# A hybrid decoder layer on one core: three sets of small transposes move from TensorE to VectorE and DRAM

## The chip, the core and the metric

The kernel runs on one core of one Trainium2 chip. The metric is the device time of one execution in microseconds (us), taken as the median of several runs. The profile comes from one execution that was recorded by the hardware profiler. Engines are called as the profile calls them: PE is TensorE (matmuls and transposes; PEld is the weight load that overlaps them), DVE is VectorE, ACT is ScalarE, POOL is GpSimd, SP is SyncE, which issues nearly all DMAs.

## What is computed

One decoder layer on a 1024 x 1024 activation in float32. Cut to what matters here:

```python
h = rmsnorm(x, norm1_w);  proj = h @ w_in
# mixer A: gated DeltaNet, 4 heads of 128
o_a = gated_delta_rule(qa, ka, va, g, beta)                # chunked, a state is carried on
o_a = rmsnorm(o_a, gdn_norm_w) * silu(z)                   # per head; z is a slice of proj
# mixer B: 8 heads of 64, (window, dilation) in (128,1),(512,4),(2048,16)
out = (num_0*w_0 + num_1*w_1 + num_2*w_2) / den_tot        # softmax merged over three branches
x = x + concat(o_a, o_b) @ w_out
h = rmsnorm(x, norm2_w);  u = causal_dwconv(h @ w_up);  gate, up = split(u)
x = x + (silu(gate) * up) @ w_down;  return rmsnorm(x, final_norm_w)
```

## The kernel before

**Products.** Matrix products are made of float32 factors split into a rounded high and a low part, so that one product is three matmuls of 128x128 by 128x512 (`xhi,whi`, `xlo,whi`, `xhi,wlo`). The input projection has 24 column blocks of 48 such matmuls: k, V, q, v for the two mixers, eight blocks a (queries and keys of attention), and last four blocks z (the gates of mixer A, one for each head). They are called projection matmuls below. The output projection (`ohi`, `olo`) follows, then an up-projection of 22 rounds (products P1 to P7 of each round, names T, B, A, S, pair) and a down-projection.

**What sets the order.** The program is written as generators that a planner (class `Weave`, L49) interleaves. It keeps a planned TensorE clock, and for every other engine and for the DMA queue a planned time at which it is free (`account`, L81): each operation is charged a fixed time plus a time for each element of a partition. For the DMA queue of SyncE the charge is 0.05 us + 0.00142 us for each element of a partition (L157), and what it writes is ready 2.2 us later. A generator of high priority says how long it would have to wait (`need`, L98; `until` L101 waits for a named event); until then generators of lower priority run, and the lowest are the projection's matmuls. They are what fills TensorE while softmax or a recurrence is under way on the other engines. The order on each engine is fixed when the program is built.

**Mixer A.** Chains of the gated delta rule (L844) run for four heads. A chain ends with `vtok`, tokens on partitions, scaled on GpSimd. `finish` (L913) turns it: per head eight PE transposes into two PSUM banks, two ACT copies `ot` (128x512) that multiply by the norm's weight `gw2`, and a DMA each to `mixer[h]` in DRAM. When a head's z block is done (L585 waits for the event ("o", h)), `og` is loaded from `mixer[h]` (L610) and multiplied by silu(z) (`zz`, L611). `mixer_splits` (L1119) then splits each of the eight mixer outputs into `ohi` (ACT) and `olo` (DVE). These go into the sixteen slots that the projection's `xhi`, `xlo` have held, so they can only be made when the last projection block has used a slot.

**Attention** (L946). Four pairs of heads (pi), two groups each, so eight groups n = 0 to 7, and two steps of two query blocks in a group. `advance` (L1071) is a pipeline of three stages. For a pair of blocks it issues `scores` (L958: products kT,qT, then on DVE two masked reduces per block into `sm` and its maximum, on ACT two exponentials that also sum the denominators `den`, L984); one step later `turn` (L1000: transposes `ident,sm` on PE, copies `pt`, `pb` to SBUF by DVE and ACT in halves, reciprocal of `den`, and a GpSimd copy `rd` that broadcasts the reciprocals to 128x128); one more step later `spread` (L1023: one transpose `ident,rd` for each block into bank `rb`, and after the fourth an ACT copy `rT`), `values` (L1032), `merge_classes` (L1042) and `give` (L1056: `oT` = result times `rT` on DVE, and a DMA to `mixer[4+pi]`). Scores and turned blocks share PSUM banks, so the next scores need the copies `pt`, `pb` of the blocks before.

**Second norm.** In the first round of `up` (L1316) `rms2_power` (L1236) sums squares by sixteen small products and makes 1/rms on DVE and GpSimd (`rs`, tokens on partitions); after P7 `rms2_spread` (L1245) turns it by eight PE transposes, and two DVE copies make `rstdB` (128x1024). After P7 an ACT copy (`u3`) reads the bank `pa` in which P4 goes on adding.

Of the kernel before, what the change touches and what calls it, by code (L numbers as in the profile page):

```python
# [15 lines left out]
P = 128  # L16
# [131 lines left out]
def hybrid_layer(tc, I, out):  # L148
# [110 lines left out]
    vpark = dp.tile([S, 512], F32, name="vpark")  # L259
    qpark = dp.tile([H, P, S], F32, name="qpark")  # L260
    atpark = dp.tile([H, P, S], F32, name="atpark")
    xpark = dp.tile([KT, P, S], F32, name="xpark")
    upark = dp.tile([FT, P, S], F32, name="upark")

# [267 lines left out]
    def dense():  # L532

        yield from wv.until("first")
        yield from wv.until("norms")
        wv.add(2, first_keys())

        srcs, tiles = [], 0
        for col in DENSE:
            if col[0] == "V":  # L540
                srcs += [I["wv"][j] for j in range(4)]
            else:
                srcs.append(I["wi"][tiles])
                tiles += 1
        place = [0]
        raw = [raw_weight(srcs[0])]
        nxt = [weight(None, st=raw.pop())]
        raw.append(raw_weight(srcs[1]))

        def take():  # L550
            w = nxt.pop()
            i = place[0] = place[0] + 1
            if i < len(srcs):
                nxt.append(weight(None, st=raw.pop(), spare=i >= 17))
            if i + 1 < len(srcs):
                raw.append(raw_weight(srcs[i + 1]))
            return w

        def values_by_token(g):

            banks = [bank(t) for t in ("asc", "asc", "ch", "ch")]
            for j in range(4):
                w = [t.rearrange("p (k m) -> p k m", k=2) for t in take()]
                for kk in range(2):
                    k = 2 * j + kk
                    for i, pt in enumerate(banks):
                        c = 4 * g + i
                        yield wv.need(pt, *w)
                        mm3(pt, [t[:, c * P:(c + 1) * P] for t in xs[k]], [t[:, kk, :] for t in w], k == 0, k == KT - 1)
            for i in range(0, 4, 2):  # L570
                vx = A("vx", "ev", shape=(P, 2, 512))
                for e in range(2):
                    c = 4 * g + i + e
                    ac.activation(vx[:, e, :], banks[i + e], AF.Copy, scale=rst[:, c:c + 1])
                c = 4 * g + i
                sy.dma_start(vpark[c * P:(c + 2) * P].rearrange("(e p) d -> p e d", e=2), vx)
            wv.done.add(("V", g))

        for i, col in enumerate(DENSE):
            kind, h = col[:2]  # L580
            if kind == "V":
                yield from values_by_token(h)
                continue
            if kind == "z":
                yield from wv.until(("o", h))  # L585
            w = [t.rearrange("p (k m) -> p k m", k=KT) for t in take()]
            pair = []
            for hh in range(2):
                pt = bank("hf")
                yield wv.need(pt, *w)  # L590
                for k in range(KT):
                    mm3(pt, [t[:, k, :] for t in w], [t[:, half(hh)] for t in xs[k]], k == 0, k == KT - 1)
                    yield 0.0

                pair.append(pt)
                if hh == 0:
                    xr = A("aqkv" if kind == "a" else "xr", "go" if kind == "k" else "ev")
                scaled(pair, "xr", kind == "a", t=xr, hs=(hh,))
            if kind == "k":
                T["k", h] = conv_silu(xr, 4 + h, "kT", "kT*")  # L600
                wv.add(3, kprep(h))
            elif kind == "q":
                q = conv_silu(xr, h, "qT", "qa")
                wv.add(4, qprep(h, q))
            elif kind == "v":
                v = conv_silu(xr, 8 + h, "vT", "qa")
                wv.add(4, vprep(h, v))
            elif kind == "z":
                og = gated[h] = A("og", "kT*")
                sy.dma_start(og, mixer[h])  # L610
                ve.tensor_tensor(og, og, silu2(xr, "zz"), op=OP.mult)  # L611
            else:
                sy.dma_start(apark[h, col[2]], xr)
                wv.done.add(col)
        wv.done.add("dense")
# [295 lines left out]
        wv.add(1, finish(h, vtok))  # L911

    def finish(h, osb):  # L913
        for hh in range(2):
            pt = yield from next_bank("atr", osb)
            for c in range(4):
                i = 4 * hh + c
                tp(pt[:, c * P:(c + 1) * P], osb[:, i * P:(i + 1) * P])
            ot = tile_(sp, [P, 512], F32, "ot", "t2", 2)
            ac.activation(ot, pt, AF.Copy, scale=gw2)  # L920
            sy.dma_start(mixer[h][:, half(hh)], ot)
        wv.done.add(("o", h))


# [21 lines left out]
    def attention():  # L946
        for h in range(2):
            yield from wv.until(("c", h, NCH - 1))
        mk = A("mk", "go", shape=(P, 448))
        sy.dma_start(mk, I["mk"])  # L950
        for h in range(H):
            yield from wv.until(("o", h))
        for g in range(2):
# [46 lines left out]
        def turn(pair):  # L1000
            pts = A("pt", "dv*", shape=(P, 2, 2, 256))
            for b, (it, tag) in enumerate(zip(pair, ("asc", "atr"))):
                sm, near, far, u, den = it["sm"], it["near"], it["far"], it["u"], it["den"]
                nn, nf = near // P, -(-far // P)
                pt = it["pt"] = pts[:, b]
                pps = [bank(tag) for _ in range(2)]
                pvs = [pp.rearrange("p (e i t) -> p e i t", e=2, t=64) for pp in pps]
                for e in range(2):
                    for i in range(nn + nf):
                        o = far + i * P if i < nn else (i - nn) * P  # L1010
                        for pv, rr in zip(pvs, HALVES):
                            tp(pv[:, e, i, :], sm[rr, e, o:o + P], ident[rr, rr], 0.055)
                copies = uv.tensor_copy, lambda dst, src: ua.activation(dst, src, AF.Copy)
                for pv, rr, copy in zip(pvs, HALVES, copies):
                    copy(pt.rearrange("p e (i t) -> p e i t", t=P)[:, :, :nn, rr], pv[:, :, :nn, :])
                    for i in range(nf):
                        rows = min(it["far"] - i * P, P)
                        copy(it["pb"][i][:rows, :, u, rr], pv[:rows, :, nn + i, :])
                rd = it["rd"] = tile_(sp, [P, P], F32, "rd", ("r0", "r1", "w0", "w1")[u], 1)
                uv.reciprocal(den, den)  # L1020
                po_.tensor_copy(rd.rearrange("p (e d) -> p e d", e=2), den[:, :, None].to_broadcast([P, 2, 64]))

        def spread(pair):  # L1023
            g = pair[0]["g"]
            yield wv.need(g["rb"], *[it["rd"] for it in pair])
            for it in pair:
                tp(g["rb"][:, it["u"] * P:(it["u"] + 1) * P], it["rd"])
            if pair[1]["u"] == 3:
                g["rT"] = tile_(sp, [P, 512], F32, "rT", "t2", 2)
                ac.activation(g["rT"], g["rb"], AF.Copy)  # L1030
# [40 lines left out]
        def advance(pair):  # L1071
# [3 lines left out]
            if older is not None:  # L1075
                g = older[0]["g"]
                if older[0]["u"] == 0:
                    g.update(po=bank("ch"), rb=bank("ch"))
                yield from spread(older)
            if newer is not None:  # L1080
                turn(newer)
# [9 lines left out]
        for pi in range(4):  # L1091
            q, k, vn, vc = cur
            for hh in range(2):
# [5 lines left out]
                    wv.done.add("last group")  # L1099
                for rows, b in (((slice(96, 128), 0), (slice(32, 64), 1)) if hh else ((slice(32, 64), 0),)):  # L1100
                    po_.memset(pb[b][rows, :, 0 if b < hh else 2, :], 0.0)
                g = dict(pb=pb, hh=hh, pi=pi, vc=vc)
                for u in (0, 2):
                    yield from advance([dict(n=4 * hh + i, u=i, q=q, k=k, vn=vn, pb=pb, g=g)
                                        for i in (u, u + 1)])
# [130 lines left out]
    def rms2_power():  # L1236
        ps = bank("atr")
        for c in range(NCH):
            mm(ps[:, c:c + 1], rstdB[:, c * P:(c + 1) * P], ones[:, :1], 0.215)
        rs = sp.tile([P, NCH], F32, name="rs")  # L1240
        uv.tensor_scalar(rs, ps[:, :NCH], 1.0 / 1024, EPS, op0=OP.mult, op1=OP.add)
        rsqrt(rs, rs, NCH)
        return rs

    def rms2_spread(rs):  # L1245
        for h in range(2):
            pb = bank("atr")
            for c in range(4):
                tp(pb[:, c * P:(c + 1) * P], rs[:, 4 * h + c:4 * h + c + 1].to_broadcast([P, P]))
            ve.tensor_copy(rstdB[:, half(h)], pb)  # L1250

    W = {}
    raws = {}
# [62 lines left out]
    def up(n, before):  # L1316
# [16 lines left out]
        last["u2"] = ac.activation(u2, pa, AF.Copy)  # L1333
        if before is None:
            yield from up_product(n, "P2", pd, False, ks=(3,))
            rs = rms2_power()
        else:
            yield from up_product(n, "P5", pc, True, False)
        yield from up_product(n, "P7", pa, False, False)
        if before is None:  # L1340
            rms2_spread(rs)
        else:
            pd = yield from next_bank("hf")
            yield from up_product(n, "P2", pd)
        u3 = tile_(sp, [P, 512], F32, "u3", "t2", 2)
# [345 lines left out]
```

## Time and profile before

| | |
|---|---|
| three runs | 1201.92, 1200.84, 1200.32 us; median 1200.84 |
| the profiled execution | 1200.36 us, of which 1198.6 us is the span from the first to the last instruction |
| granted TensorE clock | 0.997 |
| busy in the span | DVE 915.1 us, ACT 574.8 us, POOL 89.8 us |
| HBM | 117.68 MB read, 35.93 MB written |

Times of the trace count from the start of the span. Of the 1.8 us between the profiled execution and its span nothing is recorded. A row of the timeline gives start, duration, engine, line and operation, output <- input, elements, a count for neighbours drawn together, and in brackets how long the engine was idle before and what ended that. Matmuls overlap, so a matmul's duration is longer than the distance to the next one's start; the distance is what a matmul costs.

### The profile page before, as it was taken

The page shows a single profiled execution, that of the slowest core. Times are in us where ns is not written, and L with a number is a line of the kernel's source. Part 1 is how long each engine was busy: PE and PEld are TensorE (multiplying, and loading weights), DVE is VectorE, ACT ScalarE, POOL GpSimd, SP SyncE. Part 2 cuts the span into 40 slices and gives each one's busy share as a digit, 9 for nine tenths or more (in the row PEclk, how much of TensorE's full clock was granted, in tenths as well). Part 3 has the DMA queues.
Part 4 walks back from the last instruction along what each step waited for, and adds up shares of the span by engine and source line. Part 5 has one row for each costly group of instructions (what it writes and reads, how often), then busy time and mean ns, then how long its engine had stood idle before and what let it go on. Part 6 is the DMA issues. An engine that isn't in the chain of part 4 may idle for free.

```text
span 1198.6 us, 18324 instructions
## 1 busy us (share of the span) xinstructions
PE 1187.5 (99%) x7050; PEld 983.7 (82%) x7050; DVE 915.1 (76%) x1450; ACT 574.8 (48%) x1126; POOL 89.8 (7%) x100
## 2 busy tenths in 40 slices
PE   9999999999999999999999999999999999999997
PEld 7888888888777778888888888888888888888886
DVE  7683975665355566777989888989898889999875
ACT  7275345355454443655544544445445454434441
POOL 0212010214311120000000000000000000000000
PEclk9999999999999999999999999999999999999998
DMA  7435234436634204543213223131222398557414
GB/s 237 107 95 150 85 109 127 152 113 183 224 95 124 73 28 128 180 154 110 88 54 104 90 70 106 53 106 60 99 90 69 109 371 292 192 157 229 160 53 141
DMA packets 85798, 154.80 MB, mean 129 GB/s; under 512 B 21168, under 2 KB 36304, under 8 KB 85712
## 3 DMA queue, kind: packets, MB, share of 16 engines
q1 hardware_dynamic: 84848, 152.85, 39.1%
q8 instruction: 55, 0.90, 0.3%
q10 hardware_dynamic: 864, 0.79, 0.2%
q14 instruction: 31, 0.25, 0.1%
HBM read 117.68 MB, written 35.93 MB: 128 GB/s over the span
## 4 chain that ended last, share of the span: by engine, by line
PE 95%; DVE 2%; ACT 2%; issue 1%; DMA 0%; POOL 0%; POOLq 0%; DVEq 0%; SPq 0%; ACTq 0%
PE ps L193 45%; PE pa L193 20%; PE dw L193 17%; PE pc L193 10%; PE ps L197 3%; DVE kT L142 1%; ACT sm L144 0%; DMA xt<-in_xT 0%; DVE x1h L142 0%; ACT whi L142 0%; PE pd L193 0%; DVE zz L142 0%; ACT dec L142 0%; DVE xr L142 0%; DVE rstdB L142 0%
## 5 line engine op out<-in xcount | busy, mean ns | idle before, releaser
L193 PE MATMUL dw<-pr 128*128 128x512 f32 (+1 forms) x984 | 211.3, 376 | 0.0
L193 PEld LDWEIGHTS dw<-pr 128*128 128x128 f32 x984 | 176.7, 188 | 33.6
L193 PE MATMUL ps<-xhi,whi 128*128 128x512 f32 x384 | 157.7, 411 | 0.3 <-ACT xhi L144 0.3
L193 PE MATMUL ps<-xhi,wlo 128*128 128x512 f32 x384 | 150.3, 391 | 0.0
L193 PE MATMUL ps<-xlo,whi 128*128 128x512 f32 x384 | 148.4, 390 | 0.0
L193 PE MATMUL pa<-T,pair 128*128 128x512 f32 x528 | 127.0, 389 | 0.0
L193 PEld LDWEIGHTS pa<-T,pair 128*128 128x128 f32 x528 | 99.0, 188 | 20.6
L193 PEld LDWEIGHTS ps<-xhi,whi 128*128 128x128 f32 x384 | 72.5, 189 | 19.6 <-issue 5.6
L193 PEld LDWEIGHTS ps<-xhi,wlo 128*128 128x128 f32 x384 | 72.4, 188 | 15.7
L193 PEld LDWEIGHTS ps<-xlo,whi 128*128 128x128 f32 x384 | 72.3, 188 | 12.5
L142 ACT ACTIVATE u<-pa 128x512 f32<-128x512 f32 x44 | 26.3, 598 | 107.2 <-PE pa L193 107.2
L142 DVE SCALAR_TENSOR_TENSOR y<-xu,fcw,y 128x1023 f32<-128x1023 f32 (+1 forms) x44 | 56.4, 1281 | 22.1 <-ACT y L142 22.0
L142 ACT ACTIVATE whi<-wst 128x1024 fp32r<-128x1024 f32 x36 | 38.2, 1063 | 65.4 <-PE ps L193 54.3
L193 PE MATMUL pa<-B,A 128*128 128x512 f32 x264 | 63.4, 389 | 0.0
L193 PE MATMUL pa<-T,S 128*128 128x512 f32 x264 | 63.4, 389 | 0.0
L193 PE MATMUL pc<-B,pair 128*128 128x512 f32 x264 | 63.4, 389 | 0.0
L193 PE MATMUL pc<-T,S 128*128 128x512 f32 x264 | 63.4, 389 | 0.0
L142 DVE TENSOR_TENSOR wst<-wst 128x512 f32<-128x512 f32 x88 | 60.5, 688 | 0.9
L193 PE MATMUL ps<-B,pair 128*128 128x512 f32 x252 | 60.5, 389 | 0.0
L142 POOL TENSOR_TENSOR rs<-rs,mhalf 128x2 f32<-128x2 f32 (+2 forms) x4 | 4.7, 1187 | 738.4 <-DVE rs L144 738.4
L142 ACT ACTIVATE pr<-wd 128x1024 fp32r<-128x1024 f32 x33 | 34.9, 1058 | 49.5 <-PE dw L193 37.0
L144 ACT ACTIVATE sm<-sm,mx 128x128 f32<-128x128 f32 (+7 forms) x64 | 35.4, 556 | 48.2 <-DVE mx L144 48.2
(248 smaller groups left out, 2411.1 us busy)
## 6 DMA issues: line engine op xcount, KB each, us to landing
wst<-in_wu SPq DMA_DIRECT2D x44, 512.0 KB, 3.7
wd<-in_wd SPq DMA_DIRECT2D x44, 512.0 KB, 4.5
upark<-y SPq DMA_DIRECT2D x22, 512.0 KB, 3.6
wst<-in_wi SPq DMA_DIRECT2D x21, 512.0 KB, 3.8
r<-upark SPq DMA_DIRECT2D x11, 512.0 KB, 7.5
r<-upark SPq DMA_DIRECT2D x22, 256.0 KB, 7.5
wa<-in_wd SPq DMA_DIRECT2D x22, 256.0 KB, 3.3
wst<-in_wv SPq DMA_DIRECT2D x8, 512.0 KB, 3.7
```

What stands on the lines that cost most here:

```text
L142: return getattr(eng, op)(*a, **kw)
L144: return getattr(eng, op)(*a, **kw)
L193: tc.stamp_issue_order_token(nc.tensor.matmul(dst, lhs, rhs, start=start, stop=stop, **kw).ins, TOKEN)
L197: tc.stamp_issue_order_token(nc.tensor.transpose(dst, src, ident if idt is None else idt).ins, TOKEN)
```

## The change

Three places change; the products themselves do not.

1. `finish` makes no PE transposes and no ACT copies. Per half head DVE transposes `vtok` in blocks of 32x32 (`ot`, 128x512), and four DMAs of 32 partitions put the blocks in place in `odram[h]`: each moves 512 pieces of 128 bytes, and there are 32 such DMAs in place of eight. `og` is loaded by four DMAs in place of one; `gw2` is multiplied in by the DVE operation that multiplies by silu(z).
2. In attention groups 0 to 6 the reciprocals go into a tile `dn` (128x32). There is no GpSimd copy, no transpose `ident,rd` and no ACT copy `rT`. When a group's fourth block is turned, DVE transposes `dn` in blocks, four small DMAs write it to `ddram[n]`, and two DMAs read it back broadcast to 64 partitions each, into `rT`. Group 7 keeps the old way.
3. The second norm's factors are transposed by DVE, written to `ndram` by four DMAs and read back by one DMA broadcast to 128 partitions, straight into `rstdB`.

```diff
                 og = gated[h] = A("og", "kT*")
-                sy.dma_start(og, mixer[h])
-                ve.tensor_tensor(og, og, silu2(xr, "zz"), op=OP.mult)
+                of = odram[h].rearrange("j (c a t) -> a j c t", c=NCH, a=4)
+                for a in range(4):
+                    sy.dma_start(v8(og)[32 * a:32 * a + 32], of[a])
+                ve.scalar_tensor_tensor(og, og, gw2, silu2(xr, "zz"), op0=OP.mult, op1=OP.mult)
...
     def finish(h, osb):
+        yield wv.need(osb)
         for hh in range(2):
-            pt = yield from next_bank("atr", osb)
-            for c in range(4):
-                i = 4 * hh + c
-                tp(pt[:, c * P:(c + 1) * P], osb[:, i * P:(i + 1) * P])
             ot = tile_(sp, [P, 512], F32, "ot", "t2", 2)
-            ac.activation(ot, pt, AF.Copy, scale=gw2)
-            sy.dma_start(mixer[h][:, half(hh)], ot)
+            ve.transpose(ot, osb[:, half(hh)])
+            to = odram[h].rearrange("j (f b i) -> b j f i", f=32, b=4)[:, :, 16 * hh:16 * hh + 16]
+            for b in range(4):
+                sy.dma_start(to[b], ot[32 * b:32 * b + 32].rearrange("p (f i) -> p f i", i=32))
         wv.done.add(("o", h))
...
+                g = it["g"]
+                if g["n"] < 7:
+                    uv.reciprocal(dns[g["n"] % 2][:, 2 * u:2 * u + 2], den)
+                    continue
                 rd = it["rd"] = tile_(sp, [P, P], F32, "rd", ("r0", "r1", "w0", "w1")[u], 1)
                 uv.reciprocal(den, den)
                 po_.tensor_copy(rd.rearrange("p (e d) -> p e d", e=2), den[:, :, None].to_broadcast([P, 2, 64]))
+            g = pair[0]["g"]
+            if g["n"] < 7 and pair[1]["u"] == 3:
+                dt = tile_(sp, [P, 32], F32, "dt", "dt", 2)
+                ve.transpose(dt, dns[g["n"] % 2])
+                to = ddram[g["n"]]
+                for b in range(4):
+                    sy.dma_start(to[:, 32 * b:32 * b + 32], dt[32 * b:32 * b + 8, :])
+                rT = g["rT"] = tile_(sp, [P, 512], F32, "rT", "t2", 2)
+                for e, er in enumerate(HALVES):
+                    src = to.rearrange("(u e) t -> e u t", e=2)[e]
+                    sy.dma_start(rT[er].rearrange("p (u t) -> p u t", u=4),
+                                 bass.AP(tensor=src.tensor, offset=src.offset, ap=[[0, 64]] + list(src.ap)))
...
         def spread(pair):
             g = pair[0]["g"]
+            if g["n"] < 7:
+                return
...
     def rms2_power():
...
+        dt = tile_(sp, [P, 32], F32, "dt", "dt", 2)
+        uv.transpose(dt, rs)
+        to = ndram.rearrange("(c t) -> c t", c=NCH)
+        for b in range(4):
+            sy.dma_start(to[:, 32 * b:32 * b + 32], dt[32 * b:32 * b + NCH, :])
+        sy.dma_start(rstdB, bass.AP(tensor=ndram.tensor, offset=ndram.offset, ap=[[0, P]] + list(ndram.ap)))
```

The planner sees other operations and so orders TensorE anew. Each `odram` DMA has 512 elements of a partition and is charged 0.05 + 0.00142 x 512 = 0.78 us of the queue, eight for each head.

**TensorE, the last step of attention.** These rows are the end of attention before: the last block pair's scores, the first of five projection products behind them (three rows, the four others left out), the transposes of group 7, two more projection products, and after the classes' products the projection goes on (35 products).

```order
L193 MATMUL ps<-kT,qT 128x256 x4
...
L193 MATMUL ps<-xhi,whi 128x512
...
L197 MATMUL ps<-ident,rd 128x128 x2
L197 MATMUL ps<-ident,sm 128x64 x32
L193 MATMUL ps<-pt,vn 64x128 x8
...
L197 MATMUL ps<-ident,rd 128x128 x2
L193 MATMUL ps<-pt,vn 64x128 x8
L193 MATMUL ps<-pb,vc 64x4x32 x8
L193 MATMUL ps<-pb,vc 64x2x32 x8
L193 MATMUL ps<-xhi,whi 128x512
```

The same place after the change, on the same engine, with nothing left out:

```order
L193 MATMUL ps<-kT,qT 128x256 x4
L193 MATMUL ps<-kT,qT 32x160 x8
L193 MATMUL ps<-kT,qT 32x192 x8
L197 MATMUL ps<-ident,rd 128x128 x2
L197 MATMUL ps<-ident,sm 128x64 x32
L193 MATMUL ps<-pt,vn 64x128 x8
L197 MATMUL ps<-ident,rd 128x128 x2
L193 MATMUL ps<-pt,vn 64x128 x8
L193 MATMUL ps<-pb,vc 64x4x32 x8
L193 MATMUL ps<-pb,vc 64x2x32 x8
L193 MATMUL ps<-ohi,whi 128x512
L193 MATMUL ps<-olo,whi 128x512
```

All projection matmuls are gone from here, 15 behind the last scores, 6 behind the values, and the block of 105 behind the classes' products. They stand earlier now: 87 matmuls directly ahead of the first scores, 33 behind the first transposes `ident,sm`, and 108 behind the second scores. From there on the fill is 12, 15, 9 and 12 matmuls a step as it was before, and the four z blocks end inside attention, in the step of groups 1, 3, 5 and 7 that turns blocks 4 and 5 (reduces of 352 and 384 elements). In the first round of the up-projection the twelve matmuls of P7 and the twelve of P4 now stand next to each other, where the eight transposes `ident,rs` were.

**VectorE, the same two steps.** DVE's rows from the step ahead to the last scores' reduces (`ISA sm,mx`), after the change; `xr`, `zz` and `og` belong to the last z block, `wlo` and `olo` to the output projection:

```order
L142 TENSOR_TENSOR xr<-ps,rstdB 128x512
L144 COPY pt<-ps 128x4x64
L144 COPY pb<-ps 96x2x64
L142 TENSOR_TENSOR wlo<-wst,whi 128x1024
L144 COPY pt<-ps 128x4x64
L144 COPY pb<-ps 128x2x64
L142 SCALAR_TENSOR_TENSOR zz<-zz,xr 128x1024
L142 TENSOR_TENSOR oT<-ps,rT 128x4x4x32
L142 SCALAR_TENSOR_TENSOR og<-og,gw_222,zz 128x1024
L144 ISA sm,mx<-ps,mk 128x416
...
L142 TENSOR_TENSOR olo<-og,ohi 128x1024
```

Before, `wlo`, `zz`, `og` and all `olo` of this place stood behind the attention, beside the 105 matmuls; between these copies and the reduces stood `oT` alone. ACT's rows changed in the same way: `whi`, `zz` and `ohi` now stand between the exponentials of the last steps.

**VectorE in the chains.** Behind a head's last chunk DVE has two block transposes now, and the next head's recurrence (`ct`, `wke`) is queued around them. `ct` is the state that the next chunk needs, here of head 3:

```order
L144 TENSOR_SCALAR wke<-ps,ke 128x128
L142 STREAM_TRANSPOSE ot<-vtok 128x512
L144 SCALAR_TENSOR_TENSOR ct<-ct,ge,ps 128x128
L142 STREAM_TRANSPOSE ot<-vtok 128x512
L144 SCALAR_TENSOR_TENSOR vtok<-ps,gq,vtok 128x128
```

In the order before, these rows stand without the transposes. On GpSimd a `wlo` now stands ahead of the product `vtok` of heads 2 and 3, behind which the transposes wait.

More of the change, by code (lines that the diff above doesn't have):

```diff
@@ L261, in hybrid_layer @@
     atpark = dp.tile([H, P, S], F32, name="atpark")
+    ddram = dp.tile([7, 8, P], F32, name="ddram")
+    ndram = dp.tile([S], F32, name="ndram")
+    odram = dp.tile([H, 32, 4 * S], F32, name="odram")
     xpark = dp.tile([KT, P, S], F32, name="xpark")
@@ L950, in attention @@
         sy.dma_start(mk, I["mk"])
+        dns = [tile_(sp, [P, 32], F32, "dn", f"dn{i}", 1) for i in range(2)]
+        for t in dns:
+            po_.memset(t, 1.0)
         for h in range(H):
@@ L1077, in advance @@
                 if older[0]["u"] == 0:
-                    g.update(po=bank("ch"), rb=bank("ch"))
+                    g.update(po=bank("ch"))
+                    if g["n"] == 7:
+                        g.update(rb=bank("ch"))
                 yield from spread(older)
@@ L1101, in attention @@
                     po_.memset(pb[b][rows, :, 0 if b < hh else 2, :], 0.0)
-                g = dict(pb=pb, hh=hh, pi=pi, vc=vc)
+                g = dict(pb=pb, hh=hh, pi=pi, vc=vc, n=2 * pi + hh)
                 for u in (0, 2):
@@ L1239, in rms2_power @@
             mm(ps[:, c:c + 1], rstdB[:, c * P:(c + 1) * P], ones[:, :1], 0.215)
[L1240 to L1250, printed above, removed]
+        rs = tile_(sp, [P, 32], F32, "rs", "dt", 2)
+        ve.memset(rs, 1.0)
+        uv.tensor_scalar(rs[:, :NCH], ps[:, :NCH], 1.0 / 1024, EPS, op0=OP.mult, op1=OP.add)
+        rsqrt(rs[:, :NCH], rs[:, :NCH], NCH)
+        dt = tile_(sp, [P, 32], F32, "dt", "dt", 2)
[4 more added lines that the diff above has]
+        sy.dma_start(rstdB, bass.AP(tensor=ndram.tensor, offset=ndram.offset, ap=[[0, P]] + list(ndram.ap)))
     W = {}
@@ L1335, in up @@
             yield from up_product(n, "P2", pd, False, ks=(3,))
-            rs = rms2_power()
+            rms2_power()
         else:
@@ L1339, in up @@
         yield from up_product(n, "P7", pa, False, False)
-        if before is None:
-            rms2_spread(rs)
-        else:
+        if before is not None:
             pd = yield from next_bank("hf")
```

## The prediction

> **What bounds the kernel now.** First the page: busy time, and the chain that ended last.
>
> ```profile
> PE 1187.5 (99%) x7050; PEld 983.7 (82%) x7050; DVE 915.1 (76%) x1450; ACT 574.8 (48%) x1126; POOL 89.8 (7%) x100
> ...
> PE 95%; DVE 2%; ACT 2%; issue 1%; DMA 0%; POOL 0%; POOLq 0%; DVEq 0%; SPq 0%; ACTq 0%
> ```
>
> TensorE is the bound, and it is so in every slice. Its waits, listed by releaser, are small:
>
> ```profile
> PE warm L193 <- DVE ones L142: 1.1, 1, 1.1
> PE ps L197 <- POOL rs L142: 1.1, 1, 1.1
> PE ps L193 <- ACT w L144: 0.5, 1, 0.5
> PE ps L193 <- DVE ct L144: 0.5, 1, 0.5
> ```
>
> So there are two questions: how much issue time leaves TensorE, and whether it still finds work while the softmax runs. The forecast is made against the profiled execution, 1200.36 us (span 1198.6 and 1.8 around it); the median of the runs shown, 1200.84, lies 0.48 higher.
>
> **What the removed transposes are worth.** The timeline of TensorE, at four transposes of `vtok` and at a pair `rd`:
>
> ```profile
> 300.31 0.60 PE L197 MATMUL ps<-ident,vtok 128*128 128x128 f32 x4
> 300.67 0.48 PE L193 MATMUL ps<-xhi,whi 128*128 128x512 f32 x1
> 300.98 0.40 PE L193 MATMUL ps<-xlo,whi 128*128 128x512 f32 x1
> ...
> 356.42 0.38 PE L197 MATMUL ps<-ident,rd 128*128 128x128 f32 x2
> 356.73 0.97 PE L197 MATMUL ps<-ident,sm 64*128 64x64 f32 x24
> ```
>
> The 0.60 overlaps its neighbours; from start to start four transposes take 300.67 - 300.31 = 0.36, and the first large matmul behind them takes 0.31 to the next start where the others take 0.23, so a group of four costs 0.44. The 32 `vtok` transposes are eight such groups: 8 x 0.44 = **-3.5**. A pair `rd` costs 0.31 where `sm` follows, nearer 0.22 without the change of operand; 28 go, 14 pairs, 3.1 to 4.3: **-3.5**.
>
> The Trainium skill ("VectorE: DVE Perf Modes", "The three transpose paths") gives 390 ns for a 128x128 bf16 transpose on TensorE and 311 ns on VectorE, which turns only 32x32 blocks. By an estimate from that figure the 60 transposes are worth 23 us; the trace, with its pipelined 0.36 for four, contradicts the figure as a cost in a stream.
>
> For the second norm the removal gives nothing:
>
> ```profile
> 567.08 2.97 PE L193 MATMUL pa<-T,pair 128*128 128x512 f32 x12
> 569.89 1.03 PE L197 MATMUL ps<-ident,rs 128*128 128x128 f32 x8
> 570.80 3.01 PE L193 MATMUL pa<-T,pair 128*128 128x512 f32 x12
> ...
> 570.15 0.60 ACT L142 ACTIVATE u<-pa 128x512 f32<-128x512 f32 x1 [1.29 <-PE pa L193]
> ```
>
> P7 fills bank `pa`, ACT copies it out (`u`) until 570.75, and only then may P4 add to it. The eight transposes lie in that gap; without them PE waits there for ACT, and P4 starts at about 570.8 as before. **0**, at best -1.0. What is late next is `rstdB`, which now goes through DRAM:
>
> ```profile
> 575.26 1.22 DVE L142 TENSOR_TENSOR xu<-xu,rstdB 128x1024 f32<-128x1024 f32 x1
> ...
> 582.01 0.60 ACT L142 ACTIVATE u<-pa 128x512 f32<-128x512 f32 x1 [3.22 <-PE pa L193]
> ```
>
> The page's list of DMA issues (count, size, us to landing) has the nearest transfers:
>
> ```profile
> dec<-gdram SPq DMA_DIRECT2D x4, 512.0 KB, 7.6
> mdram<-um SPq DMA_DIRECT2D x16, 32.0 KB, 2.0
> vn<-vpark SPq DMA_DIRECT2D x16, 128.0 KB, 4.0
> ```
>
> The factors leave GpSimd at 569.7; four small writes (2.0 to landing by `mdram`, the nearest in size of piece, and issued one after another) and a 512 KB broadcast (7.6 for the nearest row, `dec`) put it at 577 to 580 (a 128 KB read took 4.0). DVE stands still for 2 to 5 us before `xu`, then catches up while ACT has 3.2 us idle; matmuls that need its next outputs come about ten microseconds later. Cost 0, with an upper end of 3.
>
> **The block transposes on DVE.** Eight of 128x512 at about 0.69 (the trace has none; its 128x512 operations on SBUF and PSUM all take 0.67 to 0.69) are beside PE work, but in the chains the state `ct` of the next head queues behind them, and they behind GpSimd:
>
> ```profile
> 294.95 1.90 POOL L142 TENSOR_TENSOR vtok<-vtok,ms 128x1024 f32<-128x1024 f32 x1
> 296.81 2.38 POOL L142 TENSOR_TENSOR wlo<-wst,whi 128x1024 fp32r<-128x1024 f32 x1
> ...
> 298.72 0.35 DVE L144 SCALAR_TENSOR_TENSOR ct<-ct,ge,ps 128x128 f32<-128x128 f32 x1 [1.26 <-PE ps L193]
> ```
>
> With `wlo` ahead of head 2's product, `vtok` is ready at about 296.85 + 2.38 = 299.2; the transpose then ends 1.2 us after the moment at which `ct` ran. Nothing to 4 over the four heads; I take **+1.5**, since a single place shows a clear delay.
>
> **The cover of the softmax.** This is the large term. The last step before, TensorE, DVE and ACT:
>
> ```profile
> 430.68 1.89 PE L193 MATMUL ps<-kT,qT 64*128 64x256 f32 x40
> 432.50 0.50 PE L193 MATMUL ps<-xhi,whi 128*128 128x512 f32 x1
> ...
> 436.01 0.38 PE L197 MATMUL ps<-ident,rd 128*128 128x128 f32 x2
> 436.32 1.21 PE L197 MATMUL ps<-ident,sm 64*128 64x64 f32 x32
> 437.46 1.09 PE L193 MATMUL ps<-pt,vn 128*64 128x128 f32 x16
> ...
> 440.28 1.09 PE L193 MATMUL ps<-pt,vn 128*64 128x128 f32 x16
> ```
>
> ```profile
> 432.44 0.59 DVE L144 CUSTOM_DVE_ANT_0 sm<-ps,mk 128x416 f32<-128x416 f32 x1 [0.51 <-PE ps L193]
> ...
> 435.06 0.66 ACT L144 ACTIVATE sm<-sm,mx 128x448 f32<-128x448 f32 x1
> ```
>
> From the first reduce (432.44) to the last exponential's end (435.06 + 0.66, about 435.8) pass 3.4 us, and the 15 projection matmuls (432.50 to 436.01, 3.5) cover just that. The order after has nothing there. Bare, the last eight transposes wait 3.4 less the 1.2 that the `rd` pair and the first 24 take: 2.2 lost. But the same rows also show DVE and ACT loaded with what used to come later:
>
> ```profile
> 456.98 1.23 DVE L142 TENSOR_TENSOR wlo<-wst,whi 128x1024 fp32r<-128x1024 f32 x1 [0.23 <-ACT whi L142]
> ...
> 459.38 1.23 DVE L142 TENSOR_TENSOR og<-og,zz 128x1024 f32<-128x1024 f32 x1
> ...
> 463.05 3.50 DVE L142 TENSOR_TENSOR olo<-og,ohi 128x1024 fp32r<-128x1024 f32 x3 [0.85 <-ACT ohi L142]
> ...
> 461.95 2.96 ACT L142 ACTIVATE ohi<-og 128x1024 fp32r<-128x1024 f32 x3 [4.06 <-PE ps L193]
> ```
>
> - `wlo` (1.2) stands between two copies for which the values and the next scores wait: 1.2.
> - ACT makes one `ohi` of 1.0 ahead of the four exponentials and two of about 0.5 between them: the last exponential ends at 1.0 + 3.4 + 1.0 = 5.4 less about 0.6 that overlaps the reduces, 4.8 after the first reduce; PE, at 1.2, waits 3.6 (the 2.2 is in it).
> - Behind the transposes ACT has two more `ohi` (1.0) ahead of its copies, and DVE three `olo` of 0.7 between the copies: the values wait 1.8 for the one pair and 0.9 for the other.
> - The step before has three `olo` in its gaps, 0.5; at the end `oT`, `ohi` and `olo` of the last group are behind all that, 0.7.
>
> Together 8.7; before, this stretch had 1.0 of waits and switches. **+7.6**. The low end is 3 (the bare 2.2 and part of `wlo`: the scheduler's order may overlap better than a walk by hand), the high end 11 (each DVE operation in full).
>
> **The z blocks inside attention.** In groups 1, 3 and 5 DVE has `zz`, `oT`, `og` between the copies and the reduces, where `oT` alone was. Before, the first z block lay in such a place, and `zz` was slow beside GpSimd's `wlo`:
>
> ```profile
> 421.84 2.56 DVE L142 SCALAR_TENSOR_TENSOR zz<-zz,xr 128x1024 f32<-128x1024 f32 x1
> ...
> 428.70 0.40 PE L197 MATMUL ps<-ident,sm 64*128 64x64 f32 x6 [0.20 <-ACT sm L144]
> ...
> 420.94 2.38 POOL L142 TENSOR_TENSOR wlo<-wst,whi 128x1024 fp32r<-128x1024 f32 x1 [0.47 <-ACT whi L142]
> ```
>
> `zz` 1.2 to 2.6 and `og` 1.2 put the reduces 2.4 to 3.8 later; their slack was used up already: the transposes behind that first z block waited 0.2 for the exponentials (428.70). PE's scores run under the first 1 to 2 of the delay. I take 1.8 each for groups 1 and 3, 1.1 for group 5 (where DVE makes `wlo`, and `zz` runs alone), less 0.7 for the place that had one before: **+4.0**, between 1 and 7.
>
> **`rT` through DRAM.** By the rows above a write (2.0) and a broadcast read of 128 KB (4.0 by `vn`) make 6 from `dt` to `rT`, some 7 with their issue. The last `rd` of a group and the `oT` that needs it, before:
>
> ```profile
> 406.73 0.29 POOL L142 COPY rd<-mx 128x128 f32<-128x128 f32 x1 [0.92 <-DVE mx L144]
> ...
> 415.73 1.08 DVE L142 TENSOR_TENSOR oT<-ps,rT 128x512 f32<-128x512 f32 x1 [2.15 <-PE ps L193]
> ```
>
> That leaves 9, and about 8 from `dt`, which stands behind the first copies. Cost **0**, up to 3 where SP's queue holds other transfers in front.
>
> **Sum.** -3.5 - 3.5 + 0 + 1.5 + 7.6 + 4.0 + 0 = +6.1: 1206.5 for an execution like the profiled one, 1206.9 for the median; predicted 1207.
>
> **Rivals.**
> - *The stalls are mostly hidden, and it is faster.* For it: 99% busy says that the cover was just enough everywhere, and all engines but PE have idle time. Then the terms at their low ends, -7.0 + 3 + 1 + 0 = -3: 1197.8; with nothing lost 1193.8. It decides where the last step loses under 3 and each z block under 1. Against it: the cover of the last step is removed in full, which no slack elsewhere repairs. Chance 0.20. By the 390 ns that the Trainium skill gives ("VectorE: DVE Perf Modes", "The three transpose paths") it would come out near 1190; the rows above leave that a small part of this chance.
> - *Within 2.4 us of before*: last steps +5, z +2, chains 0 against -7.0: 1200.8. Chance 0.14.
> - *The transfers are late.* For it: 32 writes of 512 pieces of 128 bytes stand in SP's one queue with weights, and each `rT` is two trips through DRAM. If `rT` came 1.5 late in each of seven groups: +10 on top, 1217. Against: `mdram` moves pieces of that size and lands in 2.0. The Trainium skill ("DMA: Bandwidth & Descriptors", "Specifications") names 512 bytes as the least size for full rate, since smaller ones are read, modified and written; the `mdram` row does not show such a cost, and no run here shows it for 512 pieces at a time. Chance 0.14.
> - *The forecast*, +2.4 to +11 over before. Chance 0.52.
>
> **How the numbers follow.** Faster by more than 0.2% (2.4 us, about what a measurement can tell from no change) 0.20, within it 0.14, slower 0.66. The range leaves out one in ten on each side: 1196, inside the faster case, to 1217, where the late transfers centre.
>
> **What would show it.** Right: TensorE waits `ps <- ACT sm` or `<- DVE pt` of several us just before the first `ohi,whi` matmul; P4 starting at the end of `u`; longer steps where `zz` and `og` precede the reduces; `vtok` and `rd` gone with 0.36 a group of four. Wrong: the end of attention without such waits; `oT` waiting for `rT`; TensorE waiting for weights.

## The result, and the profile after

The changed kernel takes 1206.99 us (median of six runs, 1205.70 to 1208.17); the kernel before, in the same sessions, 1200.38 us (1199.86 to 1201.92). The ratio is 1.0054, 95% interval 1.0043 to 1.0065: slower by 6.6 us, the way that was forecast and near the forecast +6.1. The profiled execution after took 1207.43 us with a span of 1205.5 and a granted clock of 0.994.

TensorE is still the bound, busy for 2.4 us less. Its busy time and its waits by releaser:

```profile
PE 1185.1 (98%) x6982; PEld 979.6 (81%) x6982; DVE 916.2 (76%) x1465; ACT 565.9 (47%) x1111; POOL 81.4 (7%) x74
```

```profile
PE ps L197 <- ACT sm L144: 6.3, 10, 3.1
PE ps L193 <- ACT w L144: 1.4, 2, 0.9
PE ps L193 <- DVE ct L144: 1.1, 2, 0.7
...
PE pa L193 <- ACT u L142: 0.7, 1, 0.7
```

One new row stands out: 6.3 us of waiting for the exponentials `sm`, where 0.2 was. Most of it is in the last step of attention. TensorE there, after:

```profile
458.58 2.46 PE L193 MATMUL ps<-kT,qT 64*128 64x256 f32 x40
460.97 0.44 PE L197 MATMUL ps<-ident,rd 128*128 128x128 f32 x2
464.51 1.32 PE L197 MATMUL ps<-ident,sm 64*128 64x64 f32 x16 [3.11 <-ACT sm L144]
467.52 1.34 PE L197 MATMUL ps<-ident,sm 64*128 64x64 f32 x16 [1.69 <-ACT sm L144]
468.79 1.97 PE L193 MATMUL ps<-pt,vn 128*64 128x128 f32 x16
470.69 0.69 PE L197 MATMUL ps<-ident,rd 128*128 128x128 f32 x2
471.31 1.97 PE L193 MATMUL ps<-pt,vn 128*64 128x128 f32 x16
473.08 1.69 PE L193 MATMUL ps<-pb,vc 128*64 128x128 f32 x32
474.69 0.50 PE L193 MATMUL ps<-ohi,whi 128*128 128x512 f32 x1
```

Two waits, 3.11 and 1.69, and something the forecast did not have: the values `pt,vn` take 1.97 here, where the same sixteen took 1.09. The table by stretch (busy time of each engine, then the granted clock, DMA share and GB/s) shows why:

```profile
458.00:461.00 3.00, 2.92 (x59) 1.81 (x57) 3.00 (x5) 1.31 (x3) 0.00 (x0) 1.00 0.65 186
461.00:464.50 3.50, 0.41 (x8) 0.17 (x2) 3.50 (x9) 1.72 (x4) 0.00 (x0) 0.77 0.85 197
464.50:467.50 3.00, 1.32 (x16) 1.01 (x16) 2.86 (x8) 2.53 (x7) 0.29 (x1) 0.50 0.94 328
467.50:473.00 5.50, 5.48 (x50) 4.55 (x52) 3.87 (x10) 4.47 (x13) 0.29 (x1) 0.50 0.45 145
473.00:475.00 2.00, 2.00 (x37) 1.75 (x34) 1.22 (x3) 0.73 (x2) 0.00 (x0) 0.97 0.00 0
```

While TensorE stood idle its granted clock fell to 0.50, and it stayed there until 473. What it waited for is late on two engines. On DVE the last z block's `zz` and `og` stand ahead of the last reduces, so the first reduce starts 4.1 us behind the scores (462.66 against 458.58), where it was 1.8 before (432.44 against 430.68):

```profile
459.45 1.21 DVE L142 SCALAR_TENSOR_TENSOR zz<-zz,xr 128x1024 f32<-128x1024 f32 x1
...
461.48 1.26 DVE L142 SCALAR_TENSOR_TENSOR og<-og,gw,zz 128x1024 f32<-128x1024 f32 x1
462.66 0.58 DVE L144 CUSTOM_DVE_ANT_0 sm<-ps,mk 128x416 f32<-128x416 f32 x1
```

On ACT the splits `ohi` of the output projection now stand before and between the exponentials. The one before costs little: the first exponential starts 1.1 behind the first reduce, 0.7 before the change. The two between them make the second wait:

```profile
462.78 1.06 ACT L142 ACTIVATE ohi<-og 128x1024 fp32r<-128x1024 f32 x1 [3.47 <-DVE og L142]
463.74 0.63 ACT L144 ACTIVATE sm<-sm,mx 128x416 f32<-128x416 f32 x1
...
465.54 1.28 ACT L142 ACTIVATE ohi<-ot 128x512 fp32r<-128x512 f32 x2 [0.45 <-DMA ot<-mixer]
466.72 0.65 ACT L144 ACTIVATE sm<-sm,mx 128x448 f32<-128x448 f32 x1
...
467.37 0.66 ACT L144 ACTIVATE sm<-sm,mx 128x448 f32<-128x448 f32 x1
```

**The balance by stage.** The same work lies in another order, so starts are compared after correcting for the projection matmuls done by then, at 0.228 us each (105 of them from 442.79 to 466.74 before). The executions differ by 0.48 already at 143 us (the same products start at 142.65 and 143.13), before any edit. Before the first scores, 36 more matmuls stand in the order after.

| stage | before | after | worked out | gain or loss |
|---|---|---|---|---|
| to the first scores | 319.54 | 326.50 | 6.96 - 36 x 0.228 - 0.48 | -1.7 |
| to the last scores | 430.68 | 458.58 | 27.90 - 126 x 0.228 - 0.48 + 1.7 | +0.4 |
| last step, to the first `ohi` matmul (21 projection matmuls left out) | 12.11 - 4.79 | 16.11 | | +8.8 |
| to P4 of the first up round | 570.80 | 578.17 | 7.37 - 0.48 - 7.5 | -0.6 |
| to the end | 1198.6 | 1205.5 | 6.9 - 7.37 | -0.5 |

### The profile page after: what moved, and what is told of

Read it like the earlier page. It is cut to its first block, busy times and chain, and to the rows that moved or that the text cites. A ratio compares the mean times of both kernels' runs of the same rounds, so it can differ in the third digit from the quotient of the medians.

```text
span 1205.5 us, 18228 instructions
## 1 busy us (share of the span) xinstructions
PE 1185.1 (98%) x6982; PEld 979.6 (81%) x6982; DVE 916.2 (76%) x1465; ACT 565.9 (47%) x1111; POOL 81.4 (7%) x74
## 4 chain that ended last, share of the span: by engine, by line
PE 92%; DVE 3%; ACT 2%; DMA 1%; issue 1%; SPq 0%; POOLq 0%; POOL 0%; DVEq 0%; ACTq 0%
PE ps L193 43%; PE pa L193 20%; PE dw L193 17%; PE pc L193 10%; PE ps L197 2%; ACT sm L144 1%; DVE kT L142 1%; DMA ot<-mixer 0%; DMA xt<-in_xT 0%; SPq L142 0%; DMA x<-in_xT 0%; DVE og L142 0%; DVE oT L142 0%; DVE x1h L142 0%; DMA ddram<-dt 0%
## 5 line engine op out<-in xcount | busy, mean ns | idle before, releaser
L142 ACT ACTIVATE pr<-r 128x1024 fp32r<-128x1024 f32 (+1 forms) x44 | 36.4, 839 | 47.9 <-PE dw L193 30.7
L193 PEld LDWEIGHTS pc<-B,pair 128*128 128x128 f32 x264 | 49.6, 188 | 10.3
```

The costliest lines, as they stand in the source:

```text
L142: return getattr(eng, op)(*a, **kw)
L193: tc.stamp_issue_order_token(nc.tensor.matmul(dst, lhs, rhs, start=start, stop=stop, **kw).ins, TOKEN)
```

## The experiments

The theory: the loss comes from the order that the planner chose for part 1 (no fill at the end, other work between the softmax operations). The rival: the operations and transfers themselves (small writes, `rT` through DRAM) cost it. All kernels below compute the whole layer.

### Parts 2 and 3 without part 1

`finish` and the load of `og` as before, all else as after; the fill stays where it was before.

```diff
-            ve.transpose(ot, osb[:, half(hh)])
...
+                tp(pt[:, c * P:(c + 1) * P], osb[:, i * P:(i + 1) * P])
...
+            ac.activation(ot, pt, AF.Copy, scale=gw2)
+            sy.dma_start(mixer[h][:, half(hh)], ot)
```

> Parts 2 and 3 of the change alone (reciprocals and second norm through DRAM; finish as before). The order of the projection matmuls is that of before, 15 behind the last scores and 105 behind attention. If the loss comes from the fill that moved with part 1, this kernel is faster than before by the 28 transposes rd, 13 to 14 pairs at 0.24: about -3.3 us, near 1197. If the loss comes from transfers through DRAM that are late, it stays slower than before, 1203 or more, and oT waits for rT.

Measured 1198.98, ratio 0.9986 (0.9978 to 0.9995): faster than before, by 1.4 rather than 3.3. The direction is the theory's. In its trace an attention step without z work takes 7.08 (356.67 to 363.75) where before it took 7.32; four waits of 0.2 for exponentials take part of the sum back. The norm's row, the P7 and P4 of this kernel:

```profile
563.94 2.97 PE L193 MATMUL pa<-T,pair 128*128 128x512 f32 x12
567.66 3.02 PE L193 MATMUL pa<-T,pair 128*128 128x512 f32 x12 [0.75 <-ACT u L142]
```

From P7 to P4 are 3.72, as before (567.08 to 570.80) and after (574.45 to 578.17): the eight transposes were worth nothing, and ACT's `u` took their place.

### Part 1 alone

```diff
-            ac.activation(ot, pt, AF.Copy, scale=gw2)
+            ve.transpose(ot, osb[:, half(hh)])
```

Attention and the second norm are as before.

> Part 1 alone (finish by block transposes on VectorE and odram). The planner moves the fill as in the whole change: none is left at the end of attention. If the moved fill is the loss, slower than before: -1.2 in the chains, about +9 at the end and +3 or more in the steps with z blocks, 1209 to 1212, so slower than the whole change, which also saves the rd pairs. If parts 2 and 3 carry the loss, this kernel is within 2.4 us of before.

Measured 1214.52, ratio 1.0122 (1.0108 to 1.0136): 14.1 slower than before, more than expected. Here the planner took the fill from the last three steps (the output projection's matmuls fill the very last), so that two gaps follow each other (waits of 2.7 and 1.4 us for `sm`), with a mean clock of 0.50 to 0.82 in every stretch of 5 us from 455 to 480. So part 1, with the order that the planner makes for it, carries the loss; parts 2 and 3 by themselves carry none.

### All three parts, the fill kept

Only the planner's charge for the `odram` writes changes; the chip executes the same instructions in another order.

```diff
+    sc = Engine(wv, nc.sync, "sync", 0.02, 0.0, 0.2)
...
-                sy.dma_start(to[b], ot[32 * b:32 * b + 32].rearrange("p (f i) -> p f i", i=32))
+                sc.dma_start(to[b], ot[32 * b:32 * b + 32].rearrange("p (f i) -> p f i", i=32))
```

> All three parts, but the planner charges the odram writes 0.02 us of the queue and 0.2 us until they are done, so that the order of TensorE keeps its fill at the end of attention (15 behind the last scores, 105 behind attention, as before). The instructions are those of the change. If the order is the cause: -3.5 for the transposes of vtok, +2.3 in the chains, -3.3 for rd, about 1196, faster than before and 11 us faster than the change. If the instructions and transfers themselves cost the time, it stays at 1203 or more.

Measured 1199.76, ratio 0.9994 (0.9984 to 1.0005): 7.2 less than the change, so the order is what cost. It is the order of all engines: with the fill, the z blocks and the splits `ohi`, `olo` are back where they were before. But the kernel only equals the one before, and 3.8 are missing against the expectation. One place shows half of that, the step in which group 0's result `oT` is made. DVE, and the DMA queue of SP ahead of it:

```profile
341.63 1.06 DVE L142 TENSOR_TENSOR oT<-ps,rT 128x512 f32<-128x512 f32 x1 [4.41 <-DMA rT<-ddram]
342.54 0.57 DVE L144 CUSTOM_DVE_ANT_0 sm<-ps,mk 128x416 f32<-128x416 f32 x1
```

```profile
320.16 7.22 SPq L142 DMA_DIRECT2D odram<-ot  x8
...
329.00 2.50 SPq L142 DMA_DIRECT2D og<-odram  x4
...
332.65 1.37 SPq L142 DMA_DIRECT2D ddram<-dt  x4
337.86 1.29 SPq L142 DMA_DIRECT2D rT<-ddram  x2
```

Head 3's eight writes hold the queue from 320.2 to 327.4, the loads of `og` follow, and the small writes of `dt`, which is ready at 330.0, are issued from 332.7 on. The queue then waits 3.7 us for these writes to land (0.9 in the change) before it reads `rT`, and the factors of group 0 reach DVE 4.4 us late. The next step's scores start 9.47 behind these (337.98 to 347.45) in place of 7.84 before. So the rival is right too, in this one place, which in the change was covered by 108 projection matmuls.

### The fill kept, group 0 the old way

```diff
-                if g["n"] < 7:
+                if 0 < g["n"] < 7:
...
-                    if g["n"] == 7:
+                    if g["n"] in (0, 7):
```

> The kernel that keeps the fill, but attention group 0 takes its reciprocals the old way (rd and transposes), as group 7 does. In the kernel that keeps the fill, rT of group 0 came 4.4 us late for DVE because SP still held the odram writes of head 3 and the og loads, and the step took 1.9 longer. If that is what ate its gain, this one is 1.3 to 1.9 faster than it (one or two rd pairs come back, 0.5): about -3.6 against before, 1196.8. If the small writes cost elsewhere too, it stays at 1198.5 or more.

Measured 1196.02, ratio 0.9971 (0.9961 to 0.9980): 3.9 faster than before and the fastest kernel of this study. The same step, TensorE's scores at its start and at its end:

```profile
340.48 1.89 PE L194 MATMUL ps<-kT,qT 64*128 64x256 f32 x40
345.93 1.21 PE L198 MATMUL ps<-ident,sm 64*128 64x64 f32 x32
347.07 1.09 PE L194 MATMUL ps<-pt,vn 128*64 128x128 f32 x16
348.10 0.93 PE L194 MATMUL ps<-kT,qT 64*128 64x128 f32 x8
```

7.62 in place of 9.47, and no wait before the transposes. So the lateness of `rT` in group 0 ate 1.9 of the gain. The gains over before differ by more, 3.3 (3.9 less 0.6); from the first scores to the last the traces show 2.05 (106.40 against 108.45), and where the rest comes from is open. The profiled execution here, 1199.55, is the slowest of nine.

### TensorE kept busy in the gap

To the change, transposes of the identity into a spare bank: 36 behind the last scores, 16 between the two halves of the last block transposes.

```diff
+                if pair[0]["g"]["n"] == 7 and pair[0]["u"] == 2:
+                    spare = bank("hf")
+                    for i in range(36):
+                        tp(spare[:, :P], ident, us=0.0)
```

> The change, with 36 transposes of the identity behind the last scores and 16 between the two halves of the last block transposes, into a spare bank, read by nobody; they add no wait and take about the 4.8 us for which TensorE stands idle there. If the halved granted clock behind that idle time is due to the idle time, the clock stays at 1.0 and the end of attention is about 2.5 us shorter than in the change, near 1204.5. If it has another cause, the clock is still halved, and the time is that of the change or up to 1 us more, 1207 to 1208.

Measured 1210.76, ratio 1.0084 (1.0071 to 1.0096): neither value. It doesn't answer the question, since it changed more than was meant. The order on ACT moved with it: two `ohi` now stand between the two blocks' copies, and wait for a load.

```profile
472.57 1.27 ACT L142 ACTIVATE ohi<-ot 128x512 fp32r<-128x512 f32 x2 [0.95 <-DMA ot<-mixer]
473.75 0.36 ACT L144 ACTIVATE pt<-ps 128x256 f32<-128x256 f32 x1
```

On DVE the last copies stand behind the `olo` of these, and TensorE waits 2.5 us for them. The profiled execution was also 1.9 late already at 143 us (145.07 against 143.13), which no edit touches. The next two kernels put the question again with the splits held in place.

### The splits behind the softmax

The change, with `ohi`, `olo` of the last `og` and of the attention outputs ordered behind the last copies.

```diff
+            if i == 3:
+                yield from wv.until("attention")
...
+                    lo = split(src[:, sl] if i < 7 or h == 0 else last["oT"], *[t[:, sl] for t in ots[i]])
+                    after(last["whi"], last["a"])
+                    after(lo, last["v"])
```

> The change, but the splits ohi and olo of the last og and of the attention outputs are held until the last copies pt, pb (an order between instructions of the same engine; nothing is left out). The fill is still gone. If the splits between the softmax operations are part of the loss, the last exponential ends 1.9 earlier (one ohi of 1.0 ahead of it and two of 0.6 between), and the copies behind it come about 1.5 earlier: the end of attention is 3 to 3.5 shorter than in the change, near 1203.7. If the missing fill alone sets it, the time is that of the change, 1207, or the splits make the output projection wait for what was gained.

Measured 1204.28, ratio 1.0036 (1.0023 to 1.0048): 2.7 less than the change. From the last scores to the first `ohi` matmul it takes 12.84 (458.33 to 471.17) where the change took 16.11. So about 3.3 of the 8.8 lost in this step are the splits between the softmax operations, a shorter stretch at half clock included; the output projection does not wait for them later.

### The same, TensorE kept busy

The kernel above with 28 and 8 transposes of the identity; the order of the last steps on DVE and ACT stays but for a few splits behind the copies.

> As the kernel with the splits held back, and 28 + 8 transposes of the identity into a spare bank behind the last scores, read by nobody, so that TensorE is busy while it waits. They end before the exponentials do. If TensorE's idle time is what halves the granted clock, the clock stays at 1.0 and the last values and products run at full speed: 1.5 to 2.5 us less than with the splits held back, near 1202. If the clock falls for another reason, the same time as with the splits held back, or up to 0.5 more.

Measured 1203.66, ratio 1.0038 (1.0024 to 1.0051): in time no difference that the intervals show. The traces do tell the mechanism. The table by stretch, first with the splits held back, then with TensorE busy as well:

```profile
464.00:466.00 2.00, 1.74 (x26) 1.26 (x28) 1.56 (x9) 2.00 (x8) 0.29 (x1) 0.69 1.03 376
466.00:468.00 2.00, 2.00 (x22) 1.88 (x24) 0.83 (x4) 1.77 (x7) 0.29 (x1) 0.50 0.30 112
```

```profile
463.00:466.00 3.00, 3.00 (x47) 2.47 (x47) 1.87 (x10) 2.64 (x11) 0.58 (x2) 1.00 0.91 342
466.00:468.00 2.00, 2.00 (x32) 1.66 (x33) 1.10 (x4) 2.00 (x5) 0.00 (x0) 1.00 0.12 46
```

With work in the gap the clock stays at 1.00, so it is the idle time that halves it. The price here is 0.66 (the step takes 12.18, 457.59 to 469.77), less than expected, since the half clock lasted only to 468. In the change it lasted from 462.9 to 473.1, and the values and the last `rd` pair alone took 2 x (1.97 - 1.09) + 0.25 = 2.0 longer.

The two kernels divide the 8.8 lost in the last step. The splits are 3.27, of which about 1.3 is half clock (2.0 less 0.66); the half clock that is left is 0.66; and 4.86 remain with neither (12.18 against 12.11 - 4.79 = 7.32 before). Of these, 2.3 are the later reduces (4.10 behind the scores in this kernel, 461.69 against 457.59, and 1.76 before), and 2.5 the projection matmuls that no longer stand beside the softmax. The division of the 4.86 is read from the traces; no kernel held back `zz` and `og` alone.

## Why the prediction was right, step by step

The forecast was +6.1 and the medians differ by 6.6. The mechanism is the one that was forecast: the last step lost its cover, and TensorE waited there for the exponentials. That the sum came so near is in part luck, since costs of the last step that were left out stand against waits that did not come.

- **Transposes of `vtok` and the chains**, forecast -3.5 + 1.5 = -2.0; measured -1.7. The block transposes took 0.67 to 0.71, as estimated, though not every 128x512 operation on DVE takes 0.67 to 0.69: `oT` takes 1.08. The place named for the delay was wrong in part. At head 2 DVE's transpose does wait for GpSimd behind `wlo`, but TensorE has slack there and doesn't wait. Its two waits are at the two heads before. The first is the queue on DVE that the forecast named: `wke`, which `w` needs, stands behind a head's transposes and `aqkv`. In the second, DVE's transpose ahead of `ct` waited 0.7 because the tile `ot` was still being written to `odram`:

```profile
286.80 0.49 PE L193 MATMUL ps<-wke,ktok 128*128 128x128 f32 x2 [0.91 <-ACT w L144]
291.21 0.49 PE L193 MATMUL ps<-ct,kT 128*128 128x128 f32 x2 [0.70 <-DVE ct L144]
```

```profile
284.61 0.70 DVE L142 STREAM_TRANSPOSE ot<-vtok 128x512 f32<-128x512 f32 x1
...
286.13 0.31 DVE L144 TENSOR_SCALAR wke<-ps,ke 128x128 f32<-128x128 f32 x1
...
290.22 0.71 DVE L142 STREAM_TRANSPOSE ot<-vtok 128x512 f32<-128x512 f32 x1 [0.71 <-DMA odram<-ot]
...
301.00 0.71 DVE L142 STREAM_TRANSPOSE ot<-vtok 128x512 f32<-128x512 f32 x1 [0.90 <-POOL vtok L142]
```

  That the `ot` ring, two tiles deep, causes the second wait is read from the trace; a kernel with a third `ot` was not tried.
- **`rd` pairs and z blocks**, forecast -3.5 + 4.0 = +0.5; measured +0.4. In most places a step without z work became about 0.24 shorter (7.32 to 7.09, 6.67 to 6.38, 6.25 to 6.06), in the last three by 0.14 at most; the eleven of them saved 2.3, and with 0.24 in each of the three steps with z work the 14 pairs saved 3.0. The three steps with z work became 1.01, 1.06 and 0.65 longer (7.84 to 8.85, 8.90 and 8.49); with the pair that each saved they lost 1.25, 1.30 and 0.89, together 3.4 where the forecast had 1.8, 1.8 and 1.1. The first of them, after, TensorE and DVE:

```profile
372.75 1.89 PE L193 MATMUL ps<-kT,qT 64*128 64x256 f32 x40
...
378.87 0.46 PE L197 MATMUL ps<-ident,sm 64*128 64x64 f32 x8 [0.17 <-ACT sm L144]
379.52 0.46 PE L197 MATMUL ps<-ident,sm 64*128 64x64 f32 x8 [0.19 <-ACT sm L144]
380.18 0.46 PE L197 MATMUL ps<-ident,sm 64*128 64x64 f32 x8 [0.19 <-ACT sm L144]
```

```profile
372.65 2.12 DVE L142 SCALAR_TENSOR_TENSOR zz<-zz,xr 128x1024 f32<-128x1024 f32 x1 [0.52 <-ACT zz L142]
...
375.59 1.26 DVE L142 SCALAR_TENSOR_TENSOR og<-og,gw,zz 128x1024 f32<-128x1024 f32 x1
376.77 0.58 DVE L144 CUSTOM_DVE_ANT_0 sm<-ps,mk 128x416 f32<-128x416 f32 x1
```

  `zz` at 2.12 and `og` put the first reduce 4.0 behind the scores' start where it was 1.8 before; the transposes then follow the exponentials one by one, in eights.
- **The last step**, forecast +7.6 over the last three steps; measured +8.8 in the last alone. (The items of the walk make 8.7, less 1.0 before: 7.7.) The waits for the exponentials are where they were said to be, 4.8 (3.11 + 1.69) where the walk had 3.6, and the missing matmuls by themselves cost 2.5 where it had 2.2. `wlo` did stand between two copies, and the scores took 2.46 in place of 1.89. Two costs were not in the walk: it starts at the first reduce and takes that to be no later than before, but `zz` and `og` of the last z block put it 2.3 later (the term for the z blocks counts groups 1, 3 and 5 alone); and the halved clock, 2.0. One item did not come: the values were to wait 2.7 for copies, and the trace shows no such wait (TensorE is busy for 5.48 of the 5.50 us from 467.5); the half clock, at which the values took longer, hides part of it. These errors are of opposite sign and cancel in part.
- **The second norm**, forecast 0, measured 0 in three kernels. DVE waited 1.67 for `rstdB`, less than the 2 to 5 given, and TensorE did not wait for what came behind it.
- **`rT` through DRAM**, forecast 0 in this order: right, no `oT` of the change waits for it. The rival of the late transfers was given its place by another kernel: with the fill kept, it costs 1.9 in group 0.
- Not foreseen: the output projection and what follows ran 1.1 shorter than before. In the order before, two of its first matmuls start 0.2 to 0.3 later than the pitch; why the rest was gained is open.

The rival "faster" fell at the point that was named for it, the last step's cover. The kernel with the fill kept and group 0 unchanged shows that the change is worth 3.9 once the order, and with it the cover, stays as it was.

## What to carry to other kernels

Where TensorE is busy for 99% of the time, taking work off it is worth the issue time of that work, and no more if what overlapped it (here ACT's copy of a bank) still ends at the same moment. Ask first what the edit does to the order: a planner that charges a transfer 0.78 us moves the filler matmuls and the work of the other engines with them, and 126 matmuls of fill in the wrong place (29 us of them) cost more than 60 transposes saved. In a walk along one step, start from what the engine has queued ahead of it, not only from its first operation. When a change loses, change the order and keep the instructions: the fill kept, 7.2 us came back, and the one queue that then was late could be seen and avoided.

## What the hardware showed

- The granted clock of TensorE fell to 0.50 about 1.5 us after its last matmul in the change, and came back 5.6 us after TensorE had gone back to work without a break, with the splits held back 3.6 us after. Each stretch at 0.50 lasted a multiple of 3.41 us: 10.24 in the change (462.90 to 473.14), 3.41 with the splits held back (464.74 to 468.15), 6.83 and 10.24 with part 1 alone. The Trainium skill ("TensorE: Matmul & The Clock Gate", "Part 1: The HAM clock gate (the 'warmup' mystery)") says that the clock is halved after an idle window of about 3.4 us and returns after one such window of sustained work. The halving, the two levels and the 3.41 agree; the idle time here was shorter, 3.1 us in all in the change and 2.7 with the splits held back.
- VectorE's block transpose of 128x512 float32 took 0.67 to 0.71 us, of 128x32 0.19 to 0.21.
- Eight `odram` writes, each of 512 pieces of 128 bytes, kept the issuing queue of SP for 4.1 to 8.1 us in the change. With the fill kept, `rT` of group 0 was late by this queue and by the 3.7 us for which the queue waited until four small writes had landed.
- Profiled executions differ by up to 3 us at the same products near 143 us (141.99 to 145.07), ahead of every edit; why is open.
